# SSD projections: all turnings of a tile in one step of the pacing queue, followed by its copies out, in place of alternating sets of turnings and copies

## The chip, the cores and the metric

The kernel runs on one core of one Trainium2 chip. The metric is the device time in microseconds, the median of several runs; lower is better. Five engines work side by side, each through its own list of instructions in order: TensorE (PE in the profile, with its weight loads as PEld), VectorE (DVE), ScalarE (ACT), GpSimd (POOL) and SyncE (SP), which issues most of the DMAs.

## What is computed

Two layers of a diffusion backbone over 1024 latent and 256 context positions, 1024 features wide: a windowed attention layer, then a bidirectional Mamba-2 (SSD) layer, with modulated RMS norms ahead of each and one norm at the end. The change lies in the SSD layer. Cut to what matters:

```python
z, xbc, dt_raw = jnp.split(h @ w_in, [SSD_WIDTH, SSD_WIDTH + SSD_CONV_DIM], axis=-1)
xbc = jax.nn.silu(centred_depthwise_conv(xbc, conv_w, conv_b))        # 5 taps over positions
xs, bm, cm = jnp.split(xbc, [SSD_WIDTH, SSD_WIDTH + SSD_GROUPS * SSD_STATE], axis=-1)
...
states = jnp.einsum('bcsgn,bcsgr,bcsgrp->bcgrpn', bm, decay_to_end, xdt)   # per chunk of 128
cb = jnp.einsum('bcqgn,bcsgn->bcqsg', cm, bm)
y_diag = jnp.einsum('bcqsg,bcqsgr,bcsgrp->bcqgrp', cb, lmat, xdt)
y_off = jnp.einsum('bcqgn,bcgrpn,bcqgr->bcqgrp', cm, h_prev, jnp.exp(a_cs))
...
u = y * silu(z); u = rms_normalize(u, per group); out = (u * norm_w) @ w_out
```

There are 8 groups of heads. Each has its own B and C (128 states each) and 256 features of x and of z. The scans run in both directions over 8 latent chunks of 128 positions and start from the final states of the two context chunks.

## The kernel before, in words

The matrix products are made from split operands: each factor is a rounded high part and a low part (`wh`, `wl`, `uH`, `uL`), and three matmuls stand for one. ScalarE makes the high part of a weight (L1030), VectorE the low part (L1034).

The attention layer comes first, up to about 755 us. The SSD layer then runs group by group. While the scan of group g goes through its 8 chunks (`slot`, L1234), the projections of group g + 1 (`front`, L1017) are woven between its instructions. Group 0's projections run ahead of the first slot, with little else beside them, from about 755 to 855 us. In the last group's slots, the output projection (`ssd_out`) takes the place of a further group's.

`front` makes four tiles of 128 features in this order: the B tile, two x tiles, the C tile; then z in two halves. A tile of 1024 latent positions takes 48 matmuls of 128x512 (L1091) into `raw`, a PSUM tile with the tag `pj2`. One `pj2` tile is 4 KB per partition; there are two of them, so the tiles and the two halves of z take turns: the first half of z uses the buffer that the second x tile had, the second half that of the C tile. B and x tiles also have 256 context positions, 24 matmuls of 128x256 (L1081) into a tile `psD`, of which there is one.

What follows a tile's matmuls is put on a queue, `post`, and not issued at once:

- `taps` (L1000): ScalarE makes the middle tap (L1003), VectorE adds four others (L1007), into `acc` (`cacc`, `cctx`, `bT` or `cT`);
- `silu` (L1011): ScalarE's tanh writes back into `raw` (L1014), VectorE multiplies into `acc` (L1015);
- `natural` (L1049), for the B and x tiles alone: TensorE turns `acc` by 128x128 blocks with the identity (a transposition, L1054) into `raw`, which is free by then, and ScalarE copies it (L1057) into `bn` or `xn`, where positions lie on the partitions. A latent tile has 8 blocks, and goes to two destinations of 4 blocks each; a context tile has 2 blocks and one destination.

`natural` gives a pair (LATE, steps). The queue (`Queue`, L68) counts the estimated cost of the matmuls issued so far. It takes one entry for each 0.5 us of that cost; an entry that is a pair is put aside, and its steps come out, in their order and in one go, when 3.0 us more of matmul cost have been issued. Where a weight is needed that isn't split yet, or at the end of a stage, the queue is drained one step at a time. All this sets the program order. When the program is built, a scheduler fixes each engine's own order from it: an instruction that comes earlier in the program goes first among those whose inputs are there by the scheduler's clock. So the order on an engine in the profile differs from the program's.

In the slot, the lines that the prediction speaks of are: L1232, the exponentials of the decay matrix M (ScalarE, four of 128x128); L1247, M times the C-B products (VectorE); L1277, the matmuls that use M and `xn`; L1308, the turning of the last chunk's result, with its copy L1309. L1194 are the matmuls of the backward states and the context states, through `psD`, from weighted inputs that GpSimd makes (L1169) from `xn`. L1125 are the matmuls of z, into a `pj2` tile.

Of the kernel before, what the change touches and what calls it, by code (L numbers as in the profile page):

```python
# [61 lines left out]
LATE = 3.0  # L62
# [49 lines left out]
class Kernel:  # L112
# [904 lines left out]
    def front(self, g, st, post, first=None, dt=None):  # L1017
# [29 lines left out]
            return lambda: weights(a["w_z"][g, q], 4, 256)  # L1047

        def natural(raw, acc, dst, o, n):  # L1049
            steps = []  # L1050

            def tr(lo, hi):
                for x in range(lo, hi):
                    nc.tensor.transpose(raw[:, x * P : (x + 1) * P], acc[:, x * P : (x + 1) * P], self.ident)  # L1054

            def ev(d, lo, hi):
                nc.scalar.copy(d[:, :, o : o + P], raw[:, lo * P : hi * P].rearrange("p (c n) -> p c n", n=P))  # L1057

            for d, lo, hi in dst:
                steps.append(lambda lo=lo, hi=hi: tr(lo, hi))  # L1060
                steps.append(lambda d=d, lo=lo, hi=hi: ev(d, lo, hi))
            return [(LATE, steps)]

        tiles = [(16 + g, "bT"), (2 * g, 0), (2 * g + 1, 1), (24 + g, "cT")]
        st["xn"] = [t(p, [P, 4, R * HP], F32, "xn4") for _ in range(2)] + [t(p, [P, NCC, R * HP], F32, "xn2")]
# [6 lines left out]
        for n, (x, kind) in enumerate(tiles):  # L1072
# [4 lines left out]
            if nat:  # L1077
                raw = t(ps, [P, 512], F32, "psD")[:, :CTX]
                for k in range(KT):
                    for y, (l, r) in enumerate(((wh, uH), (wh, uL), (wl, uH))):  # L1080
                        nc.tensor.matmul(raw, l[:, k, :], r[2][:, k, :], start=k + y == 0, stop=k == KT - 1 and y == 2)  # L1081
                        yield N256
                acc = t(pf, [P, CTX], F32, "cctx")
                post.extend(self.taps(x, raw, acc, 0, CTX, CTX) + self.silu(raw, acc) + natural(raw, acc, [(st[nat[0]][2], 0, 2)], nat[1], 2))
# [20 lines left out]
            if nat:  # L1105
                post.extend(natural(raw, acc, [(st[nat[0]][i], 4 * i, 4 * i + 4) for i in range(2)], nat[1], 8))
# [558 lines left out]
```

## Time and profile before

| what | us |
|---|---|
| median of 3 runs | 1812.75 |
| lowest and highest of them | 1812.54, 1817.5 |
| the profiled execution's own time | 1817.81 |
| span of its instructions | 1816.1 |
| TensorE busy | 1745.0 (96%) |
| VectorE busy | 1180.8 (65%) |
| ScalarE busy | 866.3 (48%) |
| GpSimd busy | 798.6 (44%) |

The profile is of one execution. Its page gives each engine's busy time, the span in 40 slices with busy tenths, and groups of instructions by line. Lines of the trace name an instruction as engine, line, operation, what it writes and reads (by the program's names, without buffer numbers), its shape and how many in a row were merged. "[1.30 <-ACT xn L1057]" says that the engine had been idle for 1.30 us and that ScalarE's instruction of line 1057, which writes `xn`, is what it waited for. All the TensorE tiles with the tag `pj2` show as `pj`.

### The profile page before, as it was taken

Reading aid. Unit: us, or ns where it says so; the run is one execution under the profiler, and the core shown is the slowest. Engines: PE = TensorE matmul, PEld = TensorE weight load, DVE = VectorE, ACT = ScalarE, POOL = GpSimd, SP = SyncE. Lnnn points to the kernel's source line nnn. Section 1 sums busy time; section 2 is a strip of 40 time slices with the busy share of each in tenths; the row PEclk is TensorE's granted clock in tenths of the full one; section 3 lists DMA queues with packets and bytes.
Section 4 is the critical chain, followed back from the end, with each engine's and each line's share of the span. In section 5 each row is a group of like instructions: output and inputs, shape, how many; then the busy total and the mean of one; then the engine's idle time right before and its main releaser. Section 6 shows DMA issues by size and latency. Waiting matters only on the chain. (4 is left out here: it accounts for less than half of the span.)

```text
span 1816.1 us, 28983 instructions
## 1 busy us (share of the span) xinstructions
PE 1745.0 (96%) x10319; PEld 1500.2 (83%) x10319; DVE 1180.8 (65%) x2116; ACT 866.3 (48%) x1904; POOL 798.6 (44%) x1068
## 2 busy tenths in 40 slices
PE   6899999999999999999999999999999999999997
PEld 2697778888888887778898898989889898988886
DVE  4634426788877885684776757577675757767643
ACT  3612227777777774462444534344443434544522
POOL 2331117555575555103454545545454554554321
PEclk9999999999999999999999999999999999999998
DMA  9658856434454446222333323323333332656542
GB/s 327 230 144 258 275 177 154 111 96 105 115 151 129 122 108 220 73 52 72 75 74 82 92 70 86 79 76 77 81 93 73 82 79 77 185 163 179 165 135 70
DMA packets 212495, 227.61 MB, mean 125 GB/s; under 512 B 16384, under 2 KB 149632, under 8 KB 212352
## 3 DMA queue, kind: packets, MB, share of 16 engines
q1 hardware_dynamic: 178288, 207.12, 38.4%
q0 software_dynamic: 34064, 18.65, 5.7%
q8 instruction: 81, 1.33, 0.3%
q14 instruction: 62, 0.51, 0.1%
HBM read 190.88 MB, written 35.13 MB: 124 GB/s over the span
## 5 line engine op out<-in xcount | busy, mean ns | idle before, releaser
L246 PE MATMUL pj<-uH,wh 128*128 128x512 f32 (+1 forms) x712 | 259.3, 366 | 10.9 <-ACT uH L466 6.3
L247 PE MATMUL pj<-uL,wh 128*128 128x512 f32 (+1 forms) x712 | 245.1, 345 | 0.5 <-POOL uL L703 0.4
L248 PE MATMUL pj<-uH,wl 128*128 128x512 f32 (+1 forms) x712 | 244.5, 344 | 0.4 <-POOL wl L231 0.4
L1091 PE MATMUL pj<-uH,wl 128*128 128x512 f32 x512 | 172.8, 406 | 0.0
L1091 PE MATMUL pj<-uH,wh 128*128 128x512 f32 x512 | 171.5, 405 | 1.2 <-ACT bn L1057 0.7
L1091 PE MATMUL pj<-uL,wh 128*128 128x512 f32 x512 | 169.2, 403 | 0.0
L246 PEld LDWEIGHTS pj<-uH,wh 128*128 128x128 f32 x712 | 137.3, 193 | 37.8 <-ACT uH L466 7.7
L1125 PE MATMUL pj<-wh,uH 128*128 128x256 f32 x512 | 150.3, 294 | 9.1 <-ACT xn L1057 9.1
L1169 POOL TENSOR_TENSOR xw<-xn,dtdec 128x256 f32<-128x256 f32 x144 | 92.6, 648 | 141.4 <-PE psD L1194 106.8
L1125 PE MATMUL pj<-wh,uL 128*128 128x256 f32 x512 | 152.7, 298 | 0.0
L248 PEld LDWEIGHTS pj<-uH,wl 128*128 128x128 f32 x712 | 136.9, 192 | 18.4 <-issue 1.7
L247 PEld LDWEIGHTS pj<-uL,wh 128*128 128x128 f32 x712 | 137.5, 193 | 16.0 <-issue 3.0
L1125 PE MATMUL pj<-wl,uH 128*128 128x256 f32 x512 | 146.7, 286 | 0.0
L685 DVE TENSOR_TENSOR pl<-pt,ph 128x512 fp32r<-128x512 f32 x168 | 114.1, 688 | 47.3 <-ACT ph L684 46.3
L231 POOL TENSOR_TENSOR wl<-wr,wh 128x512 fp32r<-128x512 f32 x76 | 100.1, 1321 | 91.5 <-ACT wh L229 90.4
L659 DVE CUSTOM_DVE_ANT_0 sm<-S,mask,nsink 128x640 f32<-128x640 f32 (+2 forms) x160 | 119.2, 772 | 19.7 <-PE S L655 12.6
L661 ACT ACTIVATE sm<-sm,nm 128x640 f32<-128x640 f32 (+2 forms) x160 | 118.7, 742 | 16.5 <-DVE nm L659 15.8
L684 ACT CAST ph<-pt 128x512 fp32r<-128x512 f32 x168 | 97.4, 585 | 56.3 <-PE pt L680 52.9
L229 ACT CAST wh<-wr 128x512 fp32r<-128x512 f32 (+1 forms) x116 | 74.6, 648 | 92.1 <-PE pj L247 71.5
L1091 PEld LDWEIGHTS pj<-uH,wl 128*128 128x128 f32 x512 | 95.4, 188 | 19.1
L1091 PEld LDWEIGHTS pj<-uL,wh 128*128 128x128 f32 x512 | 95.5, 189 | 18.6
L1125 PEld LDWEIGHTS pj<-wh,uH 128*128 128x128 f32 x512 | 98.6, 193 | 13.5 <-ACT xn L1057 12.1
(338 smaller groups left out, 4815.9 us busy)
## 6 DMA issues: line engine op xcount, KB each, us to landing
wr<-w_x SPq DMA_DIRECT2D x32, 512.0 KB, 4.5
M<-acs SPq DMA_DIRECT2D x64, 256.0 KB, 5.0
bw<-acs SPq DMA_DIRECT2D x64, 256.0 KB, 5.4
wr<-w_sk SPq DMA_DIRECT2D x24, 512.0 KB, 3.7
wr<-wg SPq DMA_DIRECT2D x40, 256.0 KB, 4.5
qs<-q POOLq DMA_DIRECT2D x40, 256.0 KB, 3.9
wada<-w_ada SPq DMA_DIRECT2D x16, 512.0 KB, 7.2
wr<-wq SPq DMA_DIRECT2D x32, 256.0 KB, 2.8
```

What stands on the lines that cost most here:

```text
L229: nc.scalar.copy(h, raw)
L231: (eng or nc.vector).tensor_tensor(l, raw, h, op=ALU.subtract)
L246: self.nc.tensor.matmul(ps, lh, rh, start=first and i == 0, stop=False)
L247: self.nc.tensor.matmul(ps, lh, rl, start=False, stop=False)
L248: self.nc.tensor.matmul(ps, ll, rh, start=False, stop=last and i == n - 1)
L659: nc.vector.tensor_tensor_reduce(out=sm[:, :W], in0=Sv, in1=self.mask[:, m0 : m0 + W], scale=-SCALE, scalar=self.nsink[:, 4 * j + r : 4 * ...
L661: nc.scalar.activation(sm[:, :W], sm[:, :W], AF.Exp, bias=nm[:, r : r + 1], scale=-1.0, accum_out=sums[:, r : r + 1])
L684: nc.scalar.copy(ph, ptf)
L685: nc.vector.tensor_sub(pl, ptf, ph)
L1091: nc.tensor.matmul(raw[:, 512 * i : 512 * i + 512], l[:, k, :], r[i][:, k, :], start=k + y == 0, stop=k == KT - 1 and y == 2)
L1125: nc.tensor.matmul(pj[:, c], l, r[:, k, :], start=c % 2 + q + k + y == 0, stop=c % 2 == 1 and q == 1 and k == 3 and y == 2)
L1169: nc.gpsimd.tensor_tensor(xw, X(st, c).rearrange("p (r h) -> p r h", r=R), self.dtdec[:, c, hd(d, g)].unsqueeze(2).broadcast_to([P, R, HP] ...
```

## The change

In `natural`, the two alternating pairs of steps (turn four blocks, copy them; turn four blocks, copy them) become three steps: turn all blocks, then the first copy, then the second. It concerns the 24 latent tiles of B and x (three in each of 8 groups). For the context tiles, the steps are the same as before.

```diff
         def natural(raw, acc, dst, o, n):
-            steps = []
-
-            def tr(lo, hi):
-                for x in range(lo, hi):
+
+            def tr():
+                for x in range(n):
                     nc.tensor.transpose(raw[:, x * P : (x + 1) * P], acc[:, x * P : (x + 1) * P], self.ident)
 
             def ev(d, lo, hi):
                 nc.scalar.copy(d[:, :, o : o + P], raw[:, lo * P : hi * P].rearrange("p (c n) -> p c n", n=P))
 
-            for d, lo, hi in dst:
-                steps.append(lambda lo=lo, hi=hi: tr(lo, hi))
-                steps.append(lambda d=d, lo=lo, hi=hi: ev(d, lo, hi))
-            return [(LATE, steps)]
+            return [(LATE, [tr] + [lambda d=d, lo=lo, hi=hi: ev(d, lo, hi) for d, lo, hi in dst])]
```

## The prediction

> **What bounds the kernel now.** I read the page first, then the busy times by stretch, then the waits of TensorE, then the order of time around one wait.
>
> ```profile
> span 1816.1 us, 28983 instructions
> PE   6899999999999999999999999999999999999997
> ```
>
> The page's busy line has TensorE at nine tenths or more from the third slice on, so only its idle time can shrink; nothing that the change touches makes its work shorter. The stretch from 937 to 1043 us is one period of the SSD stage (one group of heads). The columns are length, then busy time with count for PE, PEld, DVE, ACT and POOL, then granted clock, DMA share and GB/s.
>
> ```profile
> 822.00:824.00 2.00, 1.76 (x6) 1.21 (x6) 0.76 (x2) 2.00 (x4) 1.18 (x2) 0.53 0.46 135
> 937.00:1043.00 106.00, 104.70 (x654) 93.91 (x654) 72.73 (x123) 45.07 (x105) 53.22 (x75) 1.00 0.31 81
> ```
>
> TensorE lacks 106.00 - 104.70 = 1.30 us of this period, VectorE 33, ScalarE 61. The waits of TensorE from 770 to 1600 us, which hold all eight groups' projections (waiting tile and line, what released it, us in total, times, longest), say where that is:
>
> ```profile
> PE pj L1125 <- ACT xn L1057: 9.1, 7, 1.3
> PE pj L1054 <- DVE cacc L1015: 2.8, 2, 2.2
> PE pj L1054 <- ACT bn L1057: 1.1, 1, 1.1
> PE pj L1091 <- ACT bn L1057: 0.7, 1, 0.7
> PE pj L1054 <- ACT xn L1057: 0.6, 1, 0.6
> PE pj L1091 <- ACT xn L1057: 0.5, 1, 0.5
> PE pj L1054 <- DVE bT L1015: 0.5, 1, 0.5
> ```
>
> Five of the seven rows, 9.1 + 1.1 + 0.7 + 0.6 + 0.5 = 12.0 us, end with a copy out of `natural` (L1057): **12.0 us is the ceiling of the direct gain.** The largest is one wait of 1.3 us in each of groups 1 to 7, before the z projection. In order of time (start, length, engine, line; idle before in brackets) it looks so in group 2:
>
> ```profile
> 1028.45 0.60 PE L1054 MATMUL pj<-ident,cacc 128*128 128x128 f32 x4
> 1029.08 0.58 ACT L1057 COPY xn<-pj 128x512 f32<-128x512 f32 x1 [4.70 <-PE pj L1054]
> 1031.63 0.60 PE L1054 MATMUL pj<-ident,cacc 128*128 128x128 f32 x4
> 1031.87 1.04 ACT L1030 CAST wh<-wr 128x1024 fp32r<-128x1024 f32 x1
> 1032.81 1.21 ACT L1003 ACTIVATE cT<-pj,cb,cw 128x1024 f32<-128x1024 f32 x1
> 1033.36 0.27 PE L1308 MATMUL psX<-ident,y 128*128 128x128 f32 x1
> 1034.31 0.58 ACT L1057 COPY xn<-pj 128x512 f32<-128x512 f32 x1
> 1034.93 0.39 PE L1125 MATMUL pj<-wh,uH 128*128 128x256 f32 x1 [1.30 <-ACT xn L1057]
> ```
>
> The first four turnings of the second x tile end at 1029.05 and are copied at once. The second four come 2.6 us later. By then ScalarE has the weight cast and the C tile's first tap before it, so the second copy ends at 1034.89. The z projection needs that tile's PSUM buffer (`pj2` has two) and starts 0.04 us after it. TensorE has been free since 1033.63.
>
> **The change, part by part.** It neither adds nor removes an instruction: in each of the 24 latent tiles (three in each of eight groups) the second four turnings come ahead of the first copy in program order, and the two copies stand together. The context tiles have one set and one copy, and stay. The moved step issues no DMA, so SP's queue gets nothing; POOL's work isn't passed either. The queue's entry has three steps instead of four with the same due time, so they come out in one go as before, unless something drains the queue step by step.
>
> *The second set's wait.* That the second four wait for the first copy is seen in group 0:
>
> ```profile
> 787.10 0.65 PE L1054 MATMUL pj<-ident,bT 128*128 128x128 f32 x4 [0.50 <-DVE bT L1015]
> 788.23 0.57 ACT L1057 COPY bn<-pj 128x512 f32<-128x512 f32 x1
> 788.86 0.66 PE L1054 MATMUL pj<-ident,bT 128*128 128x128 f32 x4 [1.11 <-ACT bn L1057]
> 789.55 0.58 ACT L1057 COPY bn<-pj 128x512 f32<-128x512 f32 x1 [0.75 <-PE pj L1054]
> 790.19 0.72 PE L1091 MATMUL pj<-uH,wh 128*128 128x512 f32 x2 [0.67 <-ACT bn L1057]
> ```
>
> They start 0.06 us after its end, with TensorE idle. With the turnings ahead of the copy that wait cannot exist. The Trainium skill ("PSUM — Partial Sum Buffer", section "PSUM bank collisions raise a hardware error") states that two engines on different banks run clean, and the sets lie 2 KB apart; by that rule no wait was needed and the change would remove nothing, which is a rival below. The row of 788.86 speaks against it.
>
> *What eight in a row cost.* Four take 0.60 us and one 0.27, so a further one takes 0.11 and eight 1.04. On TensorE 0.44 us is moved forward, not added. What lies between the old places is 0.44 us later, and behind the second set's old place nothing is. If the first copy has to wait for all eight, it too is 0.44 us later. I take that worse case.
>
> ```profile
> L1057 ACT COPY xn<-pj x32: 564/578/587, 802.9 to 1563.1; 128x512 f32<-128x512 f32 x32
> ```
>
> *Groups 1 to 7.* The eight turnings end at 1029.05 + 0.44 = 1029.49, the copies at 1030.07 and 1030.65 (0.58 each, row above, median in ns). TensorE is free at 1033.63, so the buffer is released 3.0 us before the z projection can use it. The cast that stood before the second copy cannot come ahead of it now: it started at 1031.87. The wait goes whole: 7 x 1.30 = **9.1 us**. The bounds are 0 (the copy keeps its place on ScalarE) and 9.1. Next late is nothing: the z matmuls follow the transposition of L1308 on TensorE itself.
>
> *Group 0* runs with no slots beside it, so its waits lie open. B tile: ScalarE is busy until the first copy at 788.23 anyway; both copies then end at 789.39, and the projection starts there plus 0.04, not at 790.19: 0.76 us.
>
> ```profile
> 802.87 0.59 ACT L1057 COPY xn<-pj 128x512 f32<-128x512 f32 x1 [0.31 <-PE pj L1054]
> 807.04 0.57 ACT L1057 COPY xn<-pj 128x512 f32<-128x512 f32 x1
> 807.66 0.73 PE L1091 MATMUL pj<-uH,wh 128*128 128x512 f32 x2 [0.54 <-ACT xn L1057]
> 824.40 0.57 ACT L1057 COPY xn<-pj 128x512 f32<-128x512 f32 x1
> 825.02 1.12 PE L1054 MATMUL pj<-ident,cacc 128*128 128x128 f32 x4 [0.61 <-ACT xn L1057]
> 826.17 0.58 ACT L1057 COPY xn<-pj 128x512 f32<-128x512 f32 x1 [0.93 <-PE pj L1054]
> 826.81 0.58 PE L1125 MATMUL pj<-wh,uH 128*128 128x256 f32 x1
> ```
>
> First x tile: the second copy would end at 803.46 + 0.58 + 0.44 instead of 807.61, so its 0.54 us goes whole. Second x tile: the first copy stays at 824.40, the second ends at 825.55 instead of 826.75: 1.2 us. The turnings fit ahead of that even at the half clock there (0.53 in the stretch 822 to 824). Together 0.76 + 0.54 + 1.2 = **2.5 us**, between 0 and 2.9 (the four rows of group 0). In the second x tile I take the upper end, since nothing else stands between the two copies but a 0.38 us one.
>
> The Trainium skill ("TensorE: Matmul & The Clock Gate", section "Part 4: PE-mode transpose") says that transposes don't count as work for the clock gate, which speaks against eight in a row. The rows have the clock at 1.00 over a whole period with its 1.30 us wait, and at 0.53 behind the 2.2 us wait in group 0. If the rule kept the half clock for one more of the page's windows of about 3.4 us, group 0 would lose half of that, an estimate of 1.7 us, and the sum would be 9.9 instead of 11.6.
>
> *What is delayed.* ScalarE does two copies in a row, so whatever followed the first copy is up to 0.58 + 0.44 = 1.0 us later. The tightest places are in the B tile:
>
> ```profile
> 989.50 1.27 ACT L1232 ACTIVATE M<-M,vf 128x128 f32<-128x128 f32 x4
> 990.80 0.69 DVE L1247 TENSOR_TENSOR M<-M,psX 128x512 f32<-128x512 f32 x1 [0.76 <-ACT M L1232]
> 992.63 0.37 ACT L1057 COPY bn<-psD 128x256 f32<-128x256 f32 x1
> 993.06 1.10 PE L1277 MATMUL psX<-xn,M 128*128 128x64 f32 x8
> 993.98 0.36 PE L1081 MATMUL psD<-uH,wh 128*128 128x256 f32 x1
> ```
>
> The exponentials of M run while the turnings do, ahead of the copies, and keep their place; from the end of L1247 (991.49) to the matmul that reads M there are 1.57 us. The context copy ends at 993.00 and frees `psD` 0.98 us before the next context projection. A delay of 0.58 is covered; the worst, 1.0, costs 0.04 us. I cost it at nothing; uncovered it would be 7 x 0.6 = 4 us (the price is worked out in the third rival).
>
> *The sum:* 9.1 + 2.5 = 11.6 us. The profiled execution took 1817.81, its span 1816.1 and 1.7 around it that stay: 1817.81 - 11.6 = 1806.2. It is itself the slowest shown; the three timed runs lie from 1812.54 to 1817.5 with the median at 1812.75, 5.1 below the profiled one. From the median: **1801.1 us**, 0.64% faster. About 0.3% (5.4 us) is what a measurement of this kernel can tell from no change.
>
> **The rivals.**
> 1. *The second copy keeps its place.* The order on ScalarE isn't program order, and if the cast and the C tile's tap still go first, the z projection waits as before and only group 0 gains, 0 to 2.9 us: about 1811. For it: in group 2, 4.6 us lie between the copies now (1029.66 to 1034.31), so other work does get in between. Against it: the cast wasn't ready before 1031.87, 1.2 us after the copies would be done.
> 2. *The change doesn't do what it says:* the second set's wait isn't for the copy but for something that ended with it. Then 1812.75 stays. For it: only a few tiles show the wait with TensorE idle. Against it: two such rows, 0.05 and 0.06 us behind a copy, in different tiles.
> 3. *Slower: the pair of copies goes ahead of the exponentials in the B tile.* Then these wait for the turnings (989.49 + 1.04) and two copies, until 991.69 instead of 989.50: 2.2 us late, 0.6 over the 1.57 of slack, 7 x 0.6 = 4.4 us back, still 1805.5. If a tap like L1003's (1.21 in the row of 1032.81), a weight cast like L1030's (1.04) and the context copy (0.37) go ahead of them too, they are 4.8 us late, 3.2 over, 22.6 us back: 1824. It eats the gain from 3.2 us of lateness on and is slower by over 0.3% from 4.0 on. For it: M's path has little slack there. Against it: the exponentials are ready 1 us before the turnings end.
>
> **How the numbers follow.** Forecast, with all or most of the waits gone (1798 to 1807): 0.78. Rival 1: 0.10, rival 2: 0.05, rival 3 at its full price: 0.07. The forecast and the mild form of rival 3 are faster, rivals 1 and 2 are within 0.3%: 0.78, 0.15, 0.07. The range goes from 1798 (the ceiling of 12.0 from 1812.54, less some 2 for an order that may come out better elsewhere) to 1809 (the sum from the upper of the two levels that the runs show, 1806, and some of rival 1); it leaves out rivals 2 and 3 and most of rival 1.
>
> **What would show it.** Eight turnings in a row of about 1.0 us and two copies of 0.58 back to back; the row "PE pj L1125 <- ACT xn L1057" gone; TensorE's idle time in a period near 0 and the period near 104.5 us instead of 105.8 us. The sum fails if the second copy still stands behind a cast, or if waits of L1277, L1081 or L1194 appear in the list.

## The result: slower, and the profile after

The changed kernel takes **1832.09 us** (median of 4 runs, 1826.1 to 1835.2) against 1814.79 us of the kernel before (4 runs, 1812.54 to 1817.5): a ratio of 1.009, with a 95% interval from 1.0068 to 1.0111. The prediction was 1801.1 us. The profiled execution took 1826.1 us, the fastest of the four, with a span of 1824.2. The ratios here and below compare all runs of a kernel with all runs of before that were taken beside it; before falls around two levels, about 1812 and 1817 us, so a ratio can differ from the quotient of the two medians by up to 0.002.

TensorE is busy as long as before (1744.8 us of the span, before 1745.0). The waits of TensorE from 770 to 1710 us say more (L1190 here is before's L1194, L1121 its L1125, L1056 its L1057):

```profile
PE psD L1190 <- DVE hb L1202: 6.1, 4, 2.8
PE psD L1190 <- POOL xw L1165: 4.8, 1, 4.8
PE psD L1190 <- ACT hx L1194: 2.5, 1, 2.5
...
PE pj L1121 <- ACT xn L1056: 0.9, 2, 0.6
```

**The wait that was to go is gone.** Seven waits of 1.3 us before the z projection have become 0.9 us in all. In their place stands a line that the list of before did not have: L1190, the matmuls of the states, which wait for VectorE's addition into `hb` (L1202), for ScalarE's copy `hx` and, in group 0, for GpSimd's `xw`.

The change itself looks as predicted. The second x tile of group 2 in order of time:

```profile
1018.81 0.93 PE L1053 MATMUL pj<-ident,cacc 128*128 128x128 f32 x7
1019.68 0.27 PE L1053 MATMUL pj<-ident,cacc 128*128 128x128 f32 x1
1020.15 1.06 ACT L1056 COPY xn<-pj 128x512 f32<-128x512 f32 x2
...
1024.43 0.36 PE L1121 MATMUL pj<-wh,uH 128*128 128x256 f32 x1
```

Eight turnings take 1.14 us (1018.81 to 1019.95; the forecast was 1.04), two copies stand back to back, and the z projection starts 3.2 us behind them, with no idle time in its row.

So where do the 17 us come from? The span from the first context matmul of group 0 to the end, which leaves out the attention layer (after was 6.6 us ahead there, in code that is the same, so the profiled spans lie only 8.1 us apart), splits into three stretches: to the first z projection, to the last one, and to the end. The kernel before (length, then busy time with count of PE, PEld, DVE, ACT, POOL, then clock, DMA share, GB/s):

```profile
753.06:827.00 73.94, 67.75 (x340) 55.70 (x341) 59.65 (x80) 40.42 (x81) 3.61 (x5) 0.97 0.24 56
827.00:1563.74 736.74, 727.62 (x4518) 652.50 (x4518) 501.75 (x848) 308.71 (x713) 361.68 (x506) 1.00 0.32 82
1563.74:1816.10 252.36, 236.62 (x1366) 207.82 (x1366) 143.65 (x212) 96.21 (x193) 93.26 (x108) 0.97 0.47 144
```

The kernel after:

```profile
746.44:822.09 75.65, 67.13 (x340) 55.85 (x340) 59.27 (x80) 40.15 (x81) 3.81 (x6) 0.96 0.22 60
822.09:1556.66 734.57, 725.86 (x4492) 650.81 (x4492) 489.22 (x827) 310.48 (x694) 356.17 (x496) 1.00 0.28 77
1556.66:1824.20 267.54, 242.77 (x1396) 211.12 (x1394) 149.98 (x233) 102.56 (x213) 100.26 (x118) 0.97 0.49 150
```

Together 1063.0 before and 1077.8 after, 14.7 us more. Of these, 10.95 are idle time of TensorE (42.00 against 31.05); the waits of L1190 for `hb` and `hx` above make 8.6. Group 0, where 2.5 us were to be gained, loses 1.7 (1.9 to the first z matmul itself, which stands at 826.81 in before). Groups 1 to 7, where 9.1 were to be gained, gain 2.2. **The tail, of which the prediction says nothing, loses 15.2:** from the start of the last z projection on, 30 more matmuls are left to do (1396 against 1366), and TensorE idles for 24.8 us there (267.54 - 242.77) against 15.7.

The gain in groups 1 to 7 is there at first and then fades. By periods from z to z (groups 1 to 2, 5 to 6, 6 to 7):

```profile
920.00:1024.00 104.00, 104.00 (x651) 93.78 (x651) 69.97 (x123) 45.77 (x106) 54.83 (x77) 1.00 0.30 82
...
1336.00:1442.00 106.00, 103.59 (x641) 92.50 (x640) 70.72 (x124) 45.32 (x105) 49.73 (x72) 1.00 0.27 79
1442.00:1557.00 115.00, 110.11 (x666) 96.69 (x665) 73.41 (x126) 47.38 (x107) 54.22 (x78) 0.97 0.31 80
```

TensorE's idle time in these periods is 0, 2.41 and 4.89 us (length less busy time). Before, it was 1.30 each time. Something grows from group to group. It shows in the order on TensorE. The B tile of a group has latent matmuls (L1087) and context matmuls (L1077). The latent ones start first, in group 1 and in group 7 at

```profile
849.23 0.81 PE L1087 MATMUL pj<-uH,wh 128*128 128x512 f32 x2
860.77 0.47 PE L1077 MATMUL psD<-uH,wh 128*128 128x256 f32 x1
...
1471.39 0.63 PE L1087 MATMUL pj<-uH,wh 128*128 128x512 f32 x2
...
1510.34 0.47 PE L1077 MATMUL psD<-uH,wh 128*128 128x256 f32 x1
```

The context matmuls come 11.5 us behind in group 1 and 39.0 us in group 7. In the kernel before it is 13.6 us in every group from 1 on; group 7:

```profile
1488.63 0.80 PE L1091 MATMUL pj<-uH,wh 128*128 128x512 f32 x2
...
1502.22 0.47 PE L1081 MATMUL psD<-uH,wh 128*128 128x256 f32 x1
```

This distance I call **the lag**. The context matmuls share the one buffer `psD` with the 11 state matmuls of a group, each of which needs the buffer back from the one before: a serial loop of L1190, L1202, L1190. What lags there is the whole scan. And when the projections have run ahead until their own buffers are full, the loop lies bare. Group 7, in order of time (DVE and PE rows only):

```profile
1490.36 1.27 DVE L1007 SCALAR_TENSOR_TENSOR bT<-pj,cw,bT 128x1023 f32<-128x1023 f32 x1
1490.48 0.70 PE L1190 MATMUL psD<-xw,bn 128*128 128x256 f32 x2 [1.16 <-DVE hb L1202]
1491.55 0.67 DVE L1243 TENSOR_TENSOR M<-M,psX 128x512 f32<-128x512 f32 x1
...
1492.35 0.41 DVE L1202 TENSOR_TENSOR hb<-hb,psD 128x256 f32<-128x256 f32 x1
1492.69 1.20 DVE L1132 SCALAR_TENSOR_TENSOR sz<-sz,pj 128x1024 f32<-128x1024 f32 x1
1492.81 1.22 PE L1190 MATMUL psD<-xw,bn 128*128 128x256 f32 x2 [1.63 <-DVE hb L1202]
1493.94 1.22 PE L1087 MATMUL pj<-uH,wh 128*128 128x512 f32 x2
```

VectorE makes a tap (L1007) and M (L1243) between two additions to the state, and TensorE waits 1.63 us with nothing else to do. The projections' next tile starts at 1493.94, 0.05 us after VectorE's L1132 (to 1493.89) has freed a `pj2` buffer. The clock has fallen by then (0.85 in the second row, 0.50 in the third), and that tile's first pair of matmuls takes 1.22 us, where the row of group 1 above has 0.81:

```profile
1488.00:1490.00 2.00, 0.86 (x4) 0.30 (x2) 2.00 (x4) 1.53 (x5) 1.29 (x2) 1.00 0.24 62
1490.00:1492.00 2.00, 0.70 (x2) 0.30 (x2) 2.00 (x4) 1.75 (x4) 1.49 (x3) 0.85 0.70 73
1492.00:1494.00 2.00, 1.19 (x3) 0.56 (x3) 2.00 (x6) 0.18 (x1) 0.84 (x2) 0.50 0.29 71
1494.00:1496.00 2.00, 2.00 (x6) 1.61 (x6) 2.00 (x4) 0.00 (x0) 1.32 (x3) 0.50 0.43 119
1496.00:1498.00 2.00, 2.00 (x7) 1.52 (x6) 0.91 (x2) 1.03 (x1) 0.49 (x1) 0.50 0.01 2
```

In the last three rows 5.2 us of work ran at half clock, 2.6 us more than it needs at full clock (an estimate from these rows). Over the whole stage TensorE's busy time grew by 3.8 us (1035.8 against 1032.0), though the work is the same.

### The profile page after: what moved, and what is told of

Its sections match the earlier page's. It is cut to its first block, busy times and chain, and to the rows that moved or that the text cites. A ratio compares the mean times of both kernels' runs of the same rounds, so it can differ in the third digit from the quotient of the medians.

```text
span 1824.2 us, 29000 instructions
## 1 busy us (share of the span) xinstructions
PE 1744.8 (96%) x10319; PEld 1498.6 (82%) x10319; DVE 1174.2 (64%) x2116; ACT 874.2 (48%) x1904; POOL 800.3 (44%) x1068
## 5 line engine op out<-in xcount | busy, mean ns | idle before, releaser
L1087 PE MATMUL pj<-uH,wh 128*128 128x512 f32 x512 | 171.7, 408 | 4.8 <-ACT xn L1056 1.4
L1087 PE MATMUL pj<-uH,wl 128*128 128x512 f32 x512 | 167.9, 402 | 0.3 <-DVE wl L1034 0.3
L1165 POOL TENSOR_TENSOR xw<-xn,dtdec 128x256 f32<-128x256 f32 x144 | 96.5, 676 | 162.2 <-PE psD L1190 116.4
L1087 PE MATMUL pj<-uL,wh 128*128 128x512 f32 x512 | 166.0, 400 | 0.0
L246 PEld LDWEIGHTS pj<-uH,wh 128*128 128x128 f32 x712 | 135.6, 191 | 36.6 <-issue 9.0
L1121 PE MATMUL pj<-wh,uH 128*128 128x256 f32 x512 | 151.3, 296 | 0.9 <-ACT xn L1056 0.9
L1121 PE MATMUL pj<-wl,uH 128*128 128x256 f32 x512 | 149.3, 292 | 0.0
L1121 PE MATMUL pj<-wh,uL 128*128 128x256 f32 x512 | 149.2, 291 | 0.0
L1087 PEld LDWEIGHTS pj<-uH,wh 128*128 128x128 f32 x512 | 94.5, 189 | 24.9 <-ACT xn L1056 1.9
L1087 PEld LDWEIGHTS pj<-uL,wh 128*128 128x128 f32 x512 | 96.1, 189 | 19.4
L1087 PEld LDWEIGHTS pj<-uH,wl 128*128 128x128 f32 x512 | 95.4, 189 | 20.0 <-DVE wl L1034 1.1
```

Of the source, the lines that this page charges most:

```text
L246: self.nc.tensor.matmul(ps, lh, rh, start=first and i == 0, stop=False)
L1087: nc.tensor.matmul(raw[:, 512 * i : 512 * i + 512], l[:, k, :], r[i][:, k, :], start=k + y == 0, stop=k == KT - 1 and y == 2)
L1121: nc.tensor.matmul(pj[:, c], l, r[:, k, :], start=c % 2 + q + k + y == 0, stop=c % 2 == 1 and q == 1 and k == 3 and y == 2)
L1165: nc.gpsimd.tensor_tensor(xw, X(st, c).rearrange("p (r h) -> p r h", r=R), self.dtdec[:, c, hd(d, g)].unsqueeze(2).broadcast_to([P, R, HP] ...
```

## The experiments

The theory after the traces: **with the change the projections run ahead of the context and state work, the lag grows, and the serial loop through `psD` pays for it late.** The rivals: the turnings or the pair of copies cost by themselves, in one of the tiles or in group 0; or the cost comes from where the z projection lands against the state matmuls of its own group. Expectations stand as they were written before each run, so the first ones know the theory only in part.

All results, with the lag counted in the order of TensorE's instructions: how many of a group's latent matmuls (48 a tile) stand ahead of its first context matmul, groups 1 to 7. The stage is the time from the first context matmul to the end, in the profiled execution.

| kernel | lag, groups 1 to 7 | stage, us | ratio to before (95%) |
|---|---|---|---|
| before | 48 in all | 1063.0 | 1 |
| after | 40, 53, 72, 78, 94, 96, 96 | 1077.8 | 1.009 (1.0068 to 1.0111) |
| x1_only | 52, then 47 | 1059.8 | 0.9978 (0.9962 to 0.9995) |
| bx0_only | 18, then 10 | 1066.8 | 1.0003 (0.9989 to 1.0018) |
| g0_only | 40, 47, 32, then 0 | 1068.0 | 1.0029 (1.0013 to 1.0044) |
| later_only | 48, 71, 72, 78, 94, 96, 96 | 1081.8 | 1.0089 (1.0059 to 1.012) |
| hold_z | 18, 0, 10, 0, 10, 0, 10 | 1065.7 | 1.0014 (1.0001 to 1.0028) |
| psx | 0 in all | 1056.5 | 0.9963 (0.9948 to 0.9978) |
| psx_before | 0 in all | 1081.4 | 1.0103 (1.0078 to 1.0128) |
| b_x1 | 52, 50, 71, 50, 71, 50, 71 | 1060.1 | 0.9966 (0.9951 to 0.998) |
| x0_x1 | 90, then 96 | 1087.4 | 1.0149 (1.0127 to 1.0171) |
| after_late2_5 | 90, then 96 | 1098.5 | 1.022 (1.0189 to 1.0251) |
| after_late3_5 | 40, 71, 70, 71, 70, 71, 70 | 1055.5 | **0.9953** (0.9935 to 0.9971) |
| psx_b_x1 | 0 in all | 1070.9 | 1.0055 (1.0035 to 1.0075) |
| cap48 | 40, then 48 | 1059.2 | 0.998 (0.9967 to 0.9992) |
| before_late3_5 | 48, 47, 36, 24, 10, 10, 10 | 1064.8 | 1.0001 (0.9984 to 1.0017) |

### Parts of the change alone

Four kernels apply the new `natural` to some tiles and the alternating steps to the others. One more line decides, ahead of the new return; `part` turns four blocks:

```diff
+            if o == 0:            # x1_only; bx0_only: o == P; g0_only: g > 0; later_only: g == 0
+                return [(LATE, [f for d, lo, hi in dst for f in (lambda lo=lo, hi=hi: part(lo, hi), lambda d=d, lo=lo, hi=hi: ev(d, lo, hi))])]
             return [(LATE, [tr] + [lambda d=d, lo=lo, hi=hi: ev(d, lo, hi) for d, lo, hi in dst])]
```

**The second x tile alone** (x1_only; the B tile and the first x tile alternate):

> Turnings in one step for the second x tile alone; the B tile and the first x tile alternate as before. Theory A (the 1.30 us wait of z for the second copy was a brake that held the projections to the scan's pace, and without it they run ahead): as slow as the full change, 1.007 to 1.011 of before. Theory B (the loss comes from the order in which the context and state matmuls then stand on TensorE, and is there only where a group's z begins ahead of its own first state matmul; in this kernel's built order z begins behind it in groups 1 to 7, as before): the wait goes without the loss, 0.993 to 0.999 of before, 4 to 11 us faster.

Measured: 1812.91 us against 1816.23, 0.9978. The z wait is gone, and a new one stands in its place, in the waits of TensorE from 820 to 1710 us:

```profile
PE psD L1196 <- POOL xw L1171: 5.6, 6, 0.9
```

Six waits of 0.93 us (L1196 is L1190 in this kernel) where there were seven of 1.30: the first state matmul waits for the weighted input that GpSimd makes from the same `xn`. So the direct gain was 0.4 us a group and not 1.3, as long as nothing else in the order changed. This second wait, 0.4 us behind the first, the prediction missed.

**The B tile and the first x tile alone** (bx0_only):

> The other half: the B tile and the first x tile have their turnings in one step, the second x tile alternates as before, so the second copy is late again. Theory A: the brake is there, so the time of before, 0.997 to 1.003. Theory B: in this kernel's order three state matmuls stand ahead of each z instead of one; no loss from projections running ahead; 0.997 to 1.005. If it is as slow as the full change (over 1.007), the loss is from the tiles in which nothing waited, and both are wrong.

Measured: 1817.32 us, 1.0003. The second x tile still alternates, and still pays:

```profile
PE pj L1060 <- ACT xn L1056: 8.4, 7, 1.8
```

L1060 are the turnings in two sets: the second set waits for the first copy in all seven groups. By themselves these two tiles bring nothing and cost nothing.

**Group 0 alone, and groups 1 to 7 alone** (g0_only and later_only):

> The change in group 0 alone; groups 1 to 7 alternate as before. My prediction gave group 0 a gain of 2.5 us. The trace of the changed kernel gives none: z of group 0 starts 75.7 us after the first context matmul instead of 73.8. Theory A: 0 to 3 us slower than before, 0.999 to 1.002. Theory B: the later groups' order is another one than before although nothing changed there (three state matmuls ahead of z from group 3 on), so up to 5 us either way, 0.997 to 1.003.

> The change in groups 1 to 7 alone; group 0 alternates as before. Theory A: the brake is gone in groups 1 to 7, so the loss of the full change, 1.006 to 1.011. Theory B: in this order z begins ahead of its own group's first state matmul in every group, as in the full change, so the same loss, 1.006 to 1.011. If it is no slower than before, the loss begins in group 0.

Measured: 1822.1 us, 1.0029, and 1833.26 us, 1.0089. The loss lies in groups 1 to 7; group 0 alone costs 0.3% and doesn't gain. Neither half of the tiles is slow by itself, both together are: that speaks against a price of the turnings or copies, and for something in the order.

### The order

**z held back** (hold_z). The first z matmul of each group may not go ahead of the last slot or state matmul that precedes it in the program:

```diff
+                            with self.held(i + q + c + k + y == 0):
                                 nc.tensor.matmul(pj[:, c], l, r[:, k, :], ...)
...
-                nc.tensor.matmul(s, B(st, c), flat(xw.pop(n)), start=True, stop=True)
+                self.mark = nc.tensor.matmul(s, B(st, c), flat(xw.pop(n)), start=True, stop=True)
```

> The full change, with one order edge more per group: the first z matmul may not stand on TensorE ahead of the last slot or state matmul that precedes it in the program. Nothing else changes. Theory B (the loss comes from projections that get ahead of the scan's and the context's work, so that at the end of the stage that work stands alone): the context of a group's B tile no longer falls behind its latent matmuls from group to group (11 to 39 us in the changed kernel's trace, 13.6 in every group of before), and the time is back, 0.995 to 1.004 of before. Theory C (the loss comes from the tiles themselves: pairs of copies that make the context copy and the exponentials late): still 1.006 to 1.011.

Measured: 1818.96 us against 1816.99, 1.0014. The loss of the change is gone down to 0.1%, but its gain isn't there. Here the lag is short, and slots wait for inputs:

```profile
PE psX L1254 <- POOL xw L1171: 7.1, 3, 2.4
```

**Another buffer for the states** (psx: the full change; psx_before: the kernel before, with the same edit as a control). The state matmuls write to `psX`, which has three buffers:

```diff
-                s = t(ps, [P, 512], F32, "psD")[:, :256]
+                s = t(ps, [P, 512], F32, "psX")[:, :256]
```

> The full change, with the output of the state matmuls in the ring psX of three buffers instead of the single buffer psD, which the context projections then have for themselves. Theory D (the serial loop through psD, three context tiles and eleven state matmuls a group, is what falls behind once the projections run free): the lag does not grow, and the time is that of the same edit on the kernel before (the run psx_before) or up to 0.7% below it. Theory B without D: whichever of the two has its z ahead of its own first state matmul is slower; the built orders have it behind in both, so the two within 0.4% of each other. Theory C: psx slower than psx_before by 0.6 to 1.1%.

> The kernel before with the state matmuls' output in psX: the control for psx. Theory D: the loop through psD did not bind before, so 0.995 to 1.005 of before; the ring psX is used more, which may cost up to 0.5%.

Measured: 1809.92 us, 0.9963, and 1833.75 us, 1.0103. With the edit in both, the change is worth 23.8 us. The waits of TensorE from 820 to 1710 us show it, first psx, then psx_before:

```profile
PE psX L1190 <- POOL xw L1165: 7.3, 5, 5.4
PE pj L1121 <- ACT xn L1056: 2.0, 4, 0.7
```

```profile
PE pj L1125 <- ACT xn L1057: 10.9, 8, 1.5
PE psX L1245 <- DVE dg L1262: 7.3, 7, 1.0
```

In psx no state matmul waits for VectorE's `hb` any more, and the waits of z for the copies shrink from 10.9 to 2.0 us. So the change does remove what it was said to remove. But the edit alone makes the kernel before slower by 1%, through other waits, where 0.995 to 1.005 was expected, so it isn't a clean measure of the loop's price.

**The B tile and the second x tile** (b_x1; the first x tile alternates, so `if o == 0` and not the B tile):

> Turnings in one step for the B tile and the second x tile; the first x tile alternates. In the built order z begins ahead of its own group's first state matmul in every group from 1 on, as in the full change and unlike the second x tile alone. Theory B: slower than the second x tile alone and than before, 1.003 to 1.011. Theory C (each changed tile costs by itself): the second x tile alone was 0.998 and the other two together 1.000, so 0.997 to 1.001.

Measured: 1810.48 us, 0.9966. One of the theories falls here: in this kernel too z starts ahead of the first state matmul of its own group (by 3.3 to 4.5 us; before, 2.0 us behind it), and it is fast. What counts is not that order but how it develops: the lag stays at 71 or below. The lead shows at z as well: in the late groups of the four kernels whose lag comes to 96, z starts 10 to 22 us ahead of the first state matmul of its group.

**Both x tiles** (x0_x1; the B tile alternates), and **the delay of the late steps** in the changed kernel, set to 2.5 and 3.5 (`LATE = 2.5`, `LATE = 3.5`):

> Turnings in one step for both x tiles; the B tile alternates. In the built order 96 latent matmuls, two whole tiles, stand ahead of the first context matmul in groups 2 to 7, where the changed kernel comes only at the end. Theory B2: as slow as the changed kernel or slower, 1.006 to 1.020 of before. Theory C: fewer changed tiles than the full change and one fewer than it in each group, so 0.997 to 1.006.

> The full change with LATE at 2.5: the other side of the changed kernel's 3.0. The built order has 90 to 96 latent matmuls ahead of the first context matmul from group 1 on. Theory B2: as slow as the changed kernel or slower, 1.006 to 1.020 of before, although the copies come out earlier than in it. Theory C: as the changed kernel, 1.006 to 1.011; if earlier copies help, less.

> The full change, with the pacing constant LATE at 3.5 instead of 3.0: the turnings and copies of all tiles come out 0.5 us of matmul cost later; no wait and no resource is other than in the changed kernel. Theory B2 (what loses is the lag of the context and state work behind the latent tiles when it grows, counted in the built order: latent matmuls of a group ahead of its first context matmul, 48 in every group of before, 40 to 96 growing in the changed kernel, 70 to 71 in groups 2 to 7 here): a lag that is constant and under two tiles costs nothing, 0.994 to 1.001 of before. Theory C (the turnings and pairs of copies lose by themselves): 1.006 to 1.011, as the changed kernel.

Measured: 1842.06 us, 1.0149; 1855.85 us, 1.022; and 1807.2 us against 1816.53, **0.9953**, faster than before and than the changed kernel. It is the lowest number here, though the intervals of psx and b_x1 overlap with its own. x0_x1 and after_late2_5 reach the full lag at once, two whole tiles from group 2 on, and lose most. The loop's waits in after_late2_5:

```profile
PE psD L1190 <- DVE hb L1202: 10.0, 7, 2.6
...
PE pj L1087 <- ACT wh L1030: 4.1, 6, 0.7
```

The second row shows why the lag ends at 96. There are two buffers `wh`. The third tile's weight cannot be cast before one of them is free, and that one holds the B tile's weight until its context matmuls have run; of after, the row of group 7:

```profile
1513.59 1.04 ACT L1030 CAST wh<-wr 128x1024 fp32r<-128x1024 f32 x1 [0.95 <-PE psD L1077]
```

In after_late3_5 the lag settles at 70 to 71, and the three stretches are

```profile
752.90:828.80 75.90, 67.13 (x340) 55.85 (x340) 59.29 (x80) 40.08 (x81) 3.82 (x6) 0.96 0.22 59
828.80:1550.90 722.10, 722.10 (x4508) 650.91 (x4508) 501.62 (x839) 309.37 (x704) 362.98 (x498) 1.00 0.30 82
1550.90:1808.40 257.50, 239.35 (x1379) 209.31 (x1377) 147.96 (x221) 98.55 (x202) 98.87 (x116) 0.97 0.46 143
```

Not one microsecond of TensorE's time is idle in groups 1 to 7: **the 9.1 us of the prediction.** The stretch is 14.6 us shorter than before, group 0 2.0 longer and the tail 5.1 longer, part of which is work that moved from the one to the other; together 7.5 us.

**A control of the buffer edit on a fast version** (psx_b_x1: b_x1 with the states in `psX`):

> The two edits that were faster than before, together: turnings in one step for the B tile and the second x tile (0.997 of before by itself), and the state matmuls' output in psX (0.996 with the full change). In the built order no latent matmul stands ahead of the first context matmul. Theory B2: no lag, so 0.994 to 0.999 of before. If the first x tile's wait for its copy, which psX leaves open, costs as in the control with the kernel before (1.010), 1.000 to 1.006.

Measured: 1824.59 us, 1.0055, slow where the theory had it fast; the second case of the expectation came true. The first of its TensorE waits:

```profile
PE pj L1093 <- ACT xn L1056: 5.8, 4, 1.5
```

With the lag at 0 the projections have no lead, and the alternating copies of the first x tile (L1093 is the next latent matmul) are waited for in the open. A short lag has a price as well.

**The lag alone set back** (cap48). The changed kernel with one more ordering: the first latent matmul of the first x tile may not go ahead of the B tile's last context matmul. No data, buffer or delay differs:

```diff
+                            with self.tc.issue_after(st["ctx"].ins) if n == 1 and i + k + y == 0 else ExitStack():
                                 nc.tensor.matmul(raw[:, 512 * i : 512 * i + 512], l[:, k, :], r[i][:, k, :], ...)
```

> The full change at LATE 3.0, with one order edge more per group: the first latent matmul of the first x tile may not stand on TensorE ahead of the last context matmul of the B tile. In the built order the lag is 40 in group 1 and 48 in groups 2 to 7, the value of before, where the changed kernel has 53 to 96. Theory B2: the loss of the changed kernel goes with the lag alone, and with no wait of z left the time is under that of before, 0.994 to 1.001. Theory C (the turnings in one step and the pairs of copies lose by themselves at this LATE): 1.006 to 1.011.

> The kernel before with LATE at 3.5, the control for the full change at LATE 3.5 (0.995 of before). The lag in the built order falls from 48 to 10 over the groups. If the gain of that kernel is the change's and not LATE's, this is no faster than before: 0.998 to 1.006. If LATE alone gives it: 0.993 to 0.998.

Measured: cap48 takes 1810.81 us against 1812.81, 0.998, and before_late3_5, the control that puts the kernel before at a delay of 3.5, takes 1816.28, 1.0001. So the longer delay isn't a gain of its own, and one ordering of two matmuls in each group takes the changed kernel from 1.009 to 0.998. Group 7 of cap48, 13.6 us apart as before the change:

```profile
1473.73 0.81 PE L1090 MATMUL pj<-uH,wh 128*128 128x512 f32 x2
...
1487.31 0.47 PE L1077 MATMUL psD<-uH,wh 128*128 128x256 f32 x1
```

Its stretch of groups 1 to 7:

```profile
823.00:1544.20 721.20, 721.20 (x4497) 650.01 (x4498) 493.98 (x838) 311.52 (x702) 354.75 (x498) 1.00 0.31 82
```

Again no idle time; latent tiles and context matmuls both come every 104.1 us from group 2 on, and the state matmuls (here L1193) have no wait for `hb` or `hx` in its list of waits. This settles the theory against its rivals: the turnings and copies are those of the changed kernel, and z still starts ahead of its group's first state matmul (by 5.3 us in groups 2 to 7; in after by 3.2 in group 1 and by up to 22.3 later). With the lead bounded, the loss is gone. One ordering moves what follows it too, so it is the growing lead as a whole that is shown to cost, and not each wait in it.

**What stays open.** Why the order drifts at a delay of 3.0 and settles at 3.5 was not shown: the order is fixed by a scheduler with a clock of its own, and no run here looked into it. Nor is the lag a full measure of the time: 71 costs nothing in after_late3_5, 48 in cap48 is 3.7 us slower in the stage, and short lags (hold_z, psx_b_x1, g0_only) have waits of another kind. Nor is the loop through `psD` the whole price: in x0_x1 the state matmuls wait 5.8 us for `hb` and `hx`, and z once 4.3 us for a copy.

## Why the prediction was wrong, point by point

- **"The wait goes whole: 7 x 1.30"**: right as a mechanism. The row "PE pj L1125 <- ACT xn L1057" has shrunk from 9.1 to 0.9 us, the eight turnings and the pair of copies are as described, and rivals 1 and 2 are out. As a gain it needs the right order behind it: 9.1 us of idle time in groups 1 to 7 become 8.7 in after, and 0 in after_late3_5 and cap48.
- **"Next late is nothing", and "I cost it at nothing"** under *What is delayed*: **the step that failed.** The prediction took the order on TensorE as given and asked only which instruction would start later. But the order is fixed anew for each kernel, and with both x tiles turned in one step, the delay at 3.0 and no other edit (after, later_only, x0_x1), the projections draw ahead by up to two tiles, as they don't with one of them alone (x1_only, bx0_only, b_x1). In before both streams kept a period of 105.8 us. In after, from group 1 to group 7, the first latent matmuls come 103.7 us apart on average (849.23 to 1471.39 over six groups) and the first context matmuls 108.3 (860.77 to 1510.34). So the scan falls behind, and what it owes is paid in the last groups and in the tail: +15.2 us there, where the sum has 0. Part of that is no loss but work that moved from one stretch to the next (30 matmuls); the loss is in idle time (+9.0 us in the tail) and in the half clock.
- **What was next late even without a drift**: the first state matmul's wait for GpSimd's `xw`, 0.93 us in x1_only, 0.4 short of the one removed. The prediction said that z "follow the transposition of L1308 on TensorE itself" and didn't ask what else hangs on the same copy.
- **Group 0, 2.5 us**: wrong in sign. From the first context matmul to the first of z it took 75.65 us against 73.75. The B tile's gain is there: the next latent tile starts after 36.30 us against 37.13. Behind the first x tile only 0.2 us of it are left (54.41 against 54.61), since its eight turnings start after 51.80 us, where the first four of before started after 49.12. And the end is set by another chain, that of the decay rows:

```profile
812.19 1.04 POOL L1218 TENSOR_TENSOR bw<-bw,vd 128x512 f32<-128x512 f32 x1 [73.82 <-DMA bw<-acs]
...
814.08 1.28 ACT L1228 ACTIVATE M<-M,vf 128x128 f32<-128x128 f32 x4 [7.38 <-DVE M L1222]
816.84 0.41 ACT L1056 COPY xn<-psD 128x256 f32<-128x256 f32 x1
```

  ScalarE stands 7.38 us at the exponentials, which wait for a DMA by way of GpSimd and VectorE. That chain is no later than before (L1218 starts 65.75 us after the first context matmul, before 65.96). But in before ScalarE had the second x tile's tanh behind it when the exponentials started (at 820.91); now the tanh comes after them (the row of before, then of after):

```profile
815.90 1.10 ACT L1014 ACTIVATE pj<-cacc 128x1024 f32<-128x1024 f32 x1
815.88 1.07 ACT L1014 ACTIVATE pj<-cacc 128x1024 f32<-128x1024 f32 x1
```

  The second x tile's context copy comes behind them too, and from it GpSimd makes the `xw` for which L1190 waits 4.8 us (the second row of the waits above). I had taken the rows of group 0 as if nothing but the copies stood between them.
- **Rival 3**, the slower case, named the wrong place: no wait for the B tile's M (L1273 waits 0.6 us once, for ScalarE's copy `uT`). Its sum of 1824 is near the result by chance. That "waits of L1277, L1081 or L1194 appear in the list" was named as a sign of failure, and all three appeared: L1194, now L1190, as shown, and the other two (L1273 and L1077) with one wait each, of 0.6 and 1.1 us.
- **Eight turnings and the clock**: right. The clock stays at 1.00 over the period from 920 to 1024 us with eight in a row, and in group 0 the half clock lasts about as long as before (0.50 from 815.6 to 822.4 us; before, 0.51 from 822.1 to 829.0). So the rule of the Trainium skill ("TensorE: Matmul & The Clock Gate", section "Part 4: PE-mode transpose") that the prediction weighed does no harm here.

## What to carry to other kernels

A wait, or an order of steps, on the engine that bounds the kernel may also be what keeps two streams of work in step; before costing its removal at its length, ask which stream will run ahead, what the other one's serial loop is (here one PSUM buffer between TensorE and VectorE), and how far apart the two can get. Compare the distance between the two streams at the first and at the last repetition: a loss that grows from group to group doesn't show in the group that one looks at first. When a sound change loses this way, bound the lead (one ordering per group took 1.009 to 0.998) or change the pacing (0.995) before giving it up.

## What the runs showed of the hardware

- **The clock falls without a long gap.** In a stretch where TensorE was busy for 1.56 of 4 us (1488 to 1492), with one wait of 1.16 us and the start of one of 1.63, the granted clock fell (0.85 in the row from 1490 to 1492), and it was at 0.50 for the next 6 us. It fell to 0.50 after a single wait of 2.77 us too, for some 3.4 us (0.51 and 0.64 in the rows from 1604 to 1608, 1.00 behind them):

```profile
1604.07 1.22 PE L1190 MATMUL psD<-xw,bn 128*128 128x256 f32 x2 [2.77 <-DVE hb L1202]
```

  The pair of state matmuls took 1.22 us in place of 0.70. The Trainium skill ("TensorE: Matmul & The Clock Gate", section "Why this matters for your kernels") asks for no idle gaps above about 3 us between bursts; these gaps were shorter, so the trace asks for a stricter bound: short waits close together count as well.
- **Order alone is worth 43 us.** The changed kernel with a delay of 3.5 and with one of 2.5 does the same operations on the same data; the stage takes 1055.5 us and 1098.5 us, by the order of the engines' instructions.
